# First stage of a two-layer decoder trunk: channel groups, another order of loads, and shift and scale columns ended on ScalarE

## The chip, the cores and the metric

One Trainium2 chip, one core. The time is the device time of one execution in microseconds (us); a profiled execution gives the trace. The kernel is Bass/Tile code in float32. A large product is made of three passes of a rounded type (fp32r): each operand is split into a high part and the remainder, and high x high, high x low and low x high are summed in PSUM. TensorE is PE in the profile, VectorE is DVE, ScalarE is ACT, GpSimd is POOL, and SyncE (SP), which issues nearly all DMAs, appears as SPq.

## The reference

What matters here is the head of layer 0. The conditioning vector c gives a shift and a scale for each of 1024 channels, x is modulated by them, and the result is projected:

```python
def ada_mod(c, w, b):
    m = (jax.nn.silu(c) @ w + b)[:, None, :]
    shift, scale, gate = jnp.split(m, 3, axis=-1)
    return shift, scale, 1.0 + gate
...
        shift, scale, gate = ada_mod(c, ada_w[layer, 0], ada_b[layer, 0])
        u = x * (1.0 + scale) + shift
...
            y = even_mixer(u, ev_w_in[e], ...)     # starts with proj = u @ w_in
```

x is 512 tokens x 1024 channels, the shift and scale columns of `ada_w` are 1024 x 2048 (8.4 MB), and the columns of `w_in` that the first stage multiplies are 640 of 2576, and 16 more. After it come the rest of the mixer, an MLP, an attention layer and another MLP, which the change does not touch.

## The kernel before, in words

`start` is the first stage. It goes through the 1024 channels in eight chunks of 128 (kc = 0 to 7). For a chunk, `load` issues on SyncE two DMAs of `ada_w` (tile `ast`, 512 KB each: z = 0 is the shift's columns, z = 1 the scale's, each with 128 columns for all 1024 rows), one of x (tile `x`, 256 KB) and, for every second chunk, one of `w_in` (tile `ws`, 640 KB for two chunks). `sums` makes silu(c) @ ada_w on VectorE: eight multiply-adds over the row blocks, alternating between two accumulators, and an addition (tile `mod`). `modulate` transposes x on TensorE (`pt`), sums the 128 partitions of `mod` by a product with ones (`pc`, a column of shift and one of scale), adds the bias on VectorE (`shift`, `scale`), and then on ScalarE makes u = x * scale + shift and its high part `uh`; GpSimd makes the low part `ul`. It ends with `split` of the next chunk's weights: `wh` on ScalarE, `wl` on GpSimd. `gemm(kc, 0)` is the five products of `wh` and `uh`, `gemm(kc, 1)` the twelve others, into five PSUM banks `pst` and one, `pz`.

The order of the work is written out by hand: `nc.order("tsvy")` chains the instructions of TensorE, ScalarE, VectorE and SyncE's DMAs in the order of the code, so that an instruction that waits holds up all behind it on its engine. GpSimd's order is the scheduler's. In the loop each step stands as: `load(kc + 3)`, three of the fifteen small parameter loads, `gemm(kc, 0)`, `modulate(kc + 1)`, `sums(kc + 2)`, `gemm(kc, 1)`. DMAs take eight completion semaphores in turn (named DMAHW0 to DMAHW7 in the rows of the order), so a DMA is issued only when the one eight places before it has landed. The tiles `ast` have four buffers to themselves, `ws` has two. After `start` the kernel takes weights of 1 MB each through the same two `ws` buffers (`w_dma`, `w_pre`).

Of the kernel before, what the change touches and what calls it, by code (L numbers as in the profile page):

```python
# [8 lines left out]
F32 = mybir.dt.float32  # L9
# [3 lines left out]
AF = mybir.ActivationFunctionType  # L13
# [60 lines left out]
class Trunk:  # L74
# [26 lines left out]
    def setup(self):  # L101
        nc, i, c = self.nc, self.i, self.const
        self.ident = c.tile([P, P], F32, name="ident")
        make_identity(self.tc.nc, self.ident)
        self.ones = c.tile([P, P], F32, name="ones")
        nc.vector.memset(self.ones, 1.0)
        self.ones_r = c.tile([P, P], F32R, name="ones_r")
        nc.vector.tensor_copy(self.ones_r, self.ones)
        self.eps = c.tile([P, 1], F32, name="eps")
        nc.gpsimd.memset(self.eps, LN_EPS)  # L110

        crow = c.tile([KC, P], F32, name="crow")
        nc.sync.dma_start(crow, i["c"].rearrange("o (k p) -> (o k) p", p=P))
        self.braw = self.s2("colB_raw")[:, :P]
        nc.scalar.dma_start(self.braw[:96], i["ada_b"].rearrange("l s (c p) -> (l s c) p", p=P))
        pc = self.ps()
        nc.tensor.transpose(pc[:, :KC], crow, self.ident[:KC, :KC])
        craw = c.tile([P, KC], F32, name="craw")
        nc.vector.tensor_copy(craw, pc[:, :KC])
        th = c.tile([P, KC], F32, name="cth")  # L120
        nc.scalar.activation(th, craw, AF.Tanh, scale=0.5)
        nc.vector.tensor_scalar(th, th, 0.5, 0.5, op0=ALU.mult, op1=ALU.add)
        self.cs = c.tile([P, KC], F32, name="cs")
        nc.vector.tensor_tensor(self.cs, th, craw, op=ALU.mult)

        self.shift, self.scale1 = {}, {}
        for n in range(4):
            self.shift[n] = c.tile([P, KC], F32, name=f"shift{n}")
            self.scale1[n] = c.tile([P, KC], F32, name=f"scale{n}")
        self.mod_d = {n: self.dram.tile([1, 2 * D], F32, name=f"modd{n}") for n in range(1, 4)}  # L130
        self.gate_d = {2: self.dram.tile([1, D], F32, name="gated2")}

    def ada_bias(self):
        nc, i, c = self.nc, self.i, self.const
        raw = self.braw
        pt = self.ps()
        nc.tensor.transpose(pt[:, :96], raw[:96], self.ident[:96, :96])
        self.colB = c.tile([P, 96], F32, name="colB")
        nc.vector.tensor_copy(self.colB, pt[:, :96])

    def param_loads(self):

# [437 lines left out]
    def start(self):  # L580
        nc, i = self.nc, self.i
        win = i["ev_w_in"][0]
        ada = i["ada_w"][0, 0]
        self.setup()
        self.new_u()
        acc_ps = [self.ps(f"pst{m}") for m in range(5)]
        pz = self.ps("pz")
        st, hl, mods = {}, {}, {}

        def load(kc):  # L590
            k0 = kc * P
            ast = self.u8(f"ast{kc}", F32, (2, KC, P))
            for z in range(2):
                nc.sync.dma_start(ast[:, z], ada[:, z * D + k0:z * D + k0 + P].rearrange("(r p) f -> p r f", p=P))
            xs = self.s2(f"x{kc}").rearrange("p (t f) -> p t f", t=NT)
            nc.sync.dma_start(xs, i["x"][0, :, k0:k0 + P].rearrange("(t p) f -> p t f", p=P))
            if kc % 2 == 0:
                wst = self.wp.tile([P, 2, 640], F32, tag="ws", bufs=WS_BUFS, name="ws")
                nc.sync.dma_start(wst, win[k0:k0 + 256, 0:640].rearrange("(k p) f -> p k f", p=P))
            else:  # L600
                wst = st[kc - 1][2]
            st[kc] = (ast, xs, wst)

        def sums(kc):

            ast = st[kc][0]
            mf = self.s2(f"mod{kc}")
            ma = mf.rearrange("p (a z f) -> p a z f", a=2, z=2)
            for z in (slice(0, 1), slice(1, 2)) if kc in (0, KC - 1) else (slice(0, 2),):
                for r in range(KC):  # L610
                    m, src, c = ma[:, r % 2, z], ast[:, z, r, :], self.cs[:, r:r + 1]
                    if r < 2:
                        nc.vector.tensor_scalar(m, src, c, None, op0=ALU.mult)
                    else:
                        nc.vector.scalar_tensor_tensor(m, src, c, m, op0=ALU.mult, op1=ALU.add)
            nc.vector.tensor_tensor(ma[:, 0], ma[:, 0], ma[:, 1], op=ALU.add)
            mods[kc] = ma

        def modulate(kc):
            xs = st[kc][1]  # L620
            pt = self.ps("pt")
            for t in range(NT):
                nc.tensor.transpose(pt[:, t * P:t * P + P], xs[:, t], self.ident)
            ma = mods.pop(kc)
            pc = self.ps("pc")
            for z in range(2):
                nc.tensor.matmul(pc[:, 2 * z:2 * z + 2], ma[:, 0, z], self.ones[:, 0:2], start=True, stop=True)
            nc.vector.tensor_tensor(self.shift[0][:, kc:kc + 1], pc[:, 0:1], self.colB[:, kc:kc + 1], op=ALU.add)
            nc.vector.tensor_scalar(self.scale1[0][:, kc:kc + 1], pc[:, 2:3], self.colB[:, 8 + kc:9 + kc], 1.0,
                                    op0=ALU.add, op1=ALU.add)  # L630
            u = self.s2("u32")
            sc, sh = self.scale1[0][:, kc:kc + 1], self.shift[0][:, kc:kc + 1]
            nc.scalar.activation(u, pt, AF.Identity, scale=sc, bias=sh)
            uh, ul = self.uk(kc)
            nc.scalar.copy(uh, u)
            nc.gpsimd.tensor_tensor(ul, u, uh.bitcast(F32), op=ALU.subtract)
            if kc + 1 < KC:
                split(kc + 1)

        def split(kc):  # L640
            wst = st[kc][2]
            hi = self.wp.tile([P, 640], F32R, tag="wh", name="wh")
            nc.scalar.copy(hi, wst[:, kc % 2])
            lo = self.wp.tile([P, 640], F32R, tag="wl", name="wl")
            nc.gpsimd.tensor_tensor(lo, wst[:, kc % 2], hi.bitcast(F32), op=ALU.subtract)
            hl[kc] = (hi, lo)

        def gemm(kc, part):
            hi, lo = hl.pop(kc) if part else hl[kc]
            uh, ul = self.uk(kc)  # L650
            a, z = kc == 0, kc == KC - 1
            ms = [slice(m * P, m * P + P) for m in range(5)]
            if part == 0:
# [10 lines left out]
        load(0)  # L664
        self.ada_bias()
        load(1)
        wz = self.const.tile([P, KC, 16], F32, name="wz")
        nc.sync.dma_start(wz, win[:, 2560:2576].rearrange("(k p) f -> p k f", p=P))
        load(2)
        nc.order("tsvy")  # L670
        split(0)
        sums(0)
        modulate(0)
        sums(1)
        wzs = self.const.tile([P, KC, 32], F32R, name="wzs")
        nc.vector.tensor_copy(wzs[:, :, 0:16], wz)
        nc.vector.tensor_tensor(wzs[:, :, 16:32], wz, wzs[:, :, 0:16].bitcast(F32), op=ALU.subtract)
        for kc in range(KC):
            if kc + 3 < KC:
                load(kc + 3)  # L680
            if kc == 0:
                loads = self.param_loads()
            for f in loads[3 * kc:3 * kc + 3]:
                f()
            if kc == KC - 2:
# [12 lines left out]
        return acc_ps, pz
# [843 lines left out]
```

## Time and profile before

| | us |
|---|---|
| median of 3 runs (1270.35 to 1271.96) | 1271.13 |
| the profiled execution, its own time | 1276.4 |
| its span | 1274.7 |
| TensorE busy in the span | 1226.4 |
| VectorE busy | 917.2 |
| ScalarE busy | 587.0 |
| GpSimd busy | 513.3 |

TensorE is busy 96% of the span; of the 48.3 us in which it isn't, some 20 lie in the first 70 us. The page's row of the granted clock and the windows below tell where TensorE ran at the lower of its two levels. A matmul's end is modelled, so where matmuls follow each other the start of one to the start of the next is the better measure.

### The profile page before, as it was taken

To read this page: it belongs to the slowest core of one execution; us is meant where nothing else is said; L and a number is where in the kernel's file an instruction comes from. 1 tells how busy PE (TensorE), PEld (TensorE's weight loads), DVE (VectorE), ACT (ScalarE), POOL (GpSimd) and SP (SyncE) were. 2 spreads that over 40 slices of the span, in tenths; PEclk is the share of its full clock that TensorE was granted. 3 is DMA by queue.
4 is the path that set the end of the run, shared out by engine and by line. 5 is a ranking of instruction groups with operands and counts; after the bars stand their busy time and mean duration, and the time that the engine had idled before them with its cause. 6 is when DMAs were issued, how large, how long until landed. Compare 5 with 4: busy or idle time off the path is not lost. (4 is left out here: it accounts for less than half of the span.)

```text
span 1274.7 us, 17852 instructions
## 1 busy us (share of the span) xinstructions
PE 1226.4 (96%) x6529; PEld 1044.1 (82%) x6529; DVE 917.2 (72%) x1470; ACT 587.0 (46%) x1028; POOL 513.3 (40%) x524
## 2 busy tenths in 40 slices
PE   5899899999999999999999999999899999999997
PEld 4687678888888888888999999887888788888886
DVE  7879887867878766879578878778767745543656
ACT  2376553453544443523666677752453332322321
POOL 3466421538312320376256557558438000000166
PEclk9899999999999999999999999999899999999999
DMA  9757414262775456524232232343261624232311
GB/s 282 213 198 262 169 63 157 96 225 74 248 255 195 162 198 231 178 87 118 83 101 84 67 93 67 109 165 100 83 232 67 214 66 132 71 114 81 133 33 66
DMA packets 131529, 177.51 MB, mean 139 GB/s; under 512 B 9270, under 2 KB 87764, under 8 KB 131442
## 3 DMA queue, kind: packets, MB, share of 16 engines
q1 hardware_dynamic: 131330, 176.33, 43.0%
q8 instruction: 51, 0.84, 0.3%
q14 instruction: 36, 0.29, 0.1%
q10 hardware_dynamic: 112, 0.05, 0.0%
HBM read 172.10 MB, written 4.26 MB: 138 GB/s over the span
## 5 line engine op out<-in xcount | busy, mean ns | idle before, releaser
L50 DVE TENSOR_TENSOR wl<-ws,wh 128x512 fp32r<-128x512 f32 (+1 forms) x255 | 269.8, 1083 | 69.4 <-ACT wh L50 64.7
L50 ACT CAST wh<-ws 128x1024 fp32r<-128x1024 f32 (+2 forms) x271 | 207.7, 808 | 202.1 <-PE p L50 81.4
L50 PE MATMUL p<-uh,wh 128*128 128x512 f32 (+1 forms) x576 | 206.2, 366 | 0.0
L50 PE MATMUL p<-uh,wl 128*128 128x512 f32 (+1 forms) x576 | 205.9, 365 | 0.0
L50 PE MATMUL p<-wh,hh 128*128 128x512 f32 (+1 forms) x516 | 201.0, 390 | 0.0
L50 PE MATMUL p<-wh,hl 128*128 128x512 f32 (+1 forms) x516 | 200.0, 388 | 0.0
L50 PE MATMUL p<-wl,hh 128*128 128x512 f32 (+1 forms) x516 | 199.9, 387 | 0.0
L50 PE MATMUL p<-ul,wh 128*128 128x512 f32 (+1 forms) x576 | 192.9, 366 | 0.0
L50 POOL TENSOR_TENSOR acc<-acc,ast 128x512 f32<-128x512 f32 x70 | 102.8, 1468 | 205.1 <-ACT ast L50 111.7
L50 DVE TENSOR_TENSOR h<-r 128x512 f32<-128x512 f32 x64 | 52.7, 826 | 125.9 <-ACT r L50 124.6
L50 PEld LDWEIGHTS p<-uh,wl 128*128 128x128 f32 x576 | 108.7, 189 | 17.6
L50 PEld LDWEIGHTS p<-uh,wh 128*128 128x128 f32 x576 | 108.6, 189 | 17.4
L50 PEld LDWEIGHTS p<-ul,wh 128*128 128x128 f32 x576 | 100.9, 189 | 17.3
L50 PEld LDWEIGHTS p<-wl,hh 128*128 128x128 f32 x516 | 96.9, 188 | 20.2 <-issue 0.5
L50 PEld LDWEIGHTS p<-wh,hh 128*128 128x128 f32 x516 | 96.9, 188 | 20.0 <-ACT hh L50 0.2
L50 PEld LDWEIGHTS p<-wh,hl 128*128 128x128 f32 x516 | 96.9, 188 | 19.9
L50 ACT ACTIVATE r<-p,colA 128x512 f32<-128x512 f32 x64 | 43.8, 685 | 148.4 <-PE p L50 148.1
L50 POOL TENSOR_TENSOR ws<-ws,gate 128x512 f32<-128x512 f32 x16 | 25.0, 1596 | 210.9 <-DMA ws<-in_mlp_w_dram 210.9
L50 DVE TENSOR_TENSOR Y<-Y,p 128x512 f32<-128x512 f32 x96 | 64.7, 680 | 41.0 <-PE p L50 40.3
L50 DVE SCALAR_TENSOR_TENSOR acc<-ast,cs,acc 128x512 f32<-128x512 f32 x70 | 83.8, 1198 | 14.2 <-DMA ast<-in_ada_w_dram 13.8
L50 ACT ACTIVATE ast<-ast,cs 128x512 f32<-128x512 f32 x70 | 49.8, 721 | 93.2 <-DMA ast<-in_ada_w_dram 91.1
L50 POOL TENSOR_TENSOR ul<-u,uh 128x512 fp32r<-128x512 f32 x32 | 44.5, 1403 | 82.8 <-ACT uh L50 70.0
(317 smaller groups left out, 2686.2 us busy)
## 6 DMA issues: line engine op xcount, KB each, us to landing
ws<-in_mlp_w_dram SPq DMA_DIRECT2D x64, 1024.0 KB
ast<-in_ada_w_dram SPq DMA_DIRECT2D x160, 256.0 KB
ws<-in_od_w_in_dram SPq DMA_DIRECT2D x16, 1024.0 KB
ast<-in_ada_w_dram SPq DMA_DIRECT2D x16, 512.0 KB
ws<-in_ev_w_in_dram SPq DMA_DIRECT2D x7, 1024.0 KB
ws<-in_ev_w_out_dram SPq DMA_DIRECT2D x4, 1024.0 KB
nf<-fd SPq DMA_DIRECT2D x16, 256.0 KB
ws<-in_od_w_out_dram SPq DMA_DIRECT2D x4, 1024.0 KB
```

What stands on the lines that cost most here:

```text
L50: x = f(*a, **k)
```

## The change

The eight chunks are loaded and summed in six groups: 0, 1, (2, 3), (4, 5), 6, 7. A group of two loads `ada_w` in rows of 256 columns instead of 128 (four DMAs of 512 KB into two tiles), x in rows of 256 channels, and sums with VectorE instructions of 512 elements a partition (shift and scale of two chunks) instead of 256. The shift of chunk 0 is not summed on VectorE: TensorE multiplies the eight row blocks as they were loaded with silu(c) (`cs2`). The bias additions leave VectorE: ScalarE makes each column of shift and scale from `pc` with the bias `colB` or `colB1` (bias plus one). Loads, sums, transposes, column sums and modulation become functions of their own, placed anew: the fifteen parameter loads stand together, behind group 3's loads and ahead of those of chunks 6 and 7.

```diff
+        self.cs2 = c.tile([P, KC, 2], F32, name="cs2")
+        for q in range(2):
+            nc.vector.tensor_tensor(self.cs2[:, :, q], th, craw, op=ALU.mult)
...
+        self.colB1 = c.tile([P, KC], F32, name="colB1")
+        nc.vector.tensor_scalar(self.colB1, self.colB[:, 8:16], 1.0, None, op0=ALU.add)
...
+        GROUPS = [(0,), (1,), (2, 3), (4, 5), (6,), (7,)]
...
+        def load(n):
+            g = GROUPS[n]
+            k0, w = g[0] * P, len(g) * P
+            nr = KC // len(g)
+            AST[n] = []
+            for r0 in range(0, KC, nr):
+                t = self.u8(f"ast{k0}_{r0}", F32, (2, nr, w))
+                for z in range(2):
+                    nc.sync.dma_start(t[:, z], ada[r0 * P:(r0 + nr) * P, z * D + k0:z * D + k0 + w]
+                                      .rearrange("(r p) f -> p r f", p=P))
+                AST[n] += [t[:, :, r] for r in range(nr)]
...
+        def sums(n):
+            w, zs = len(GROUPS[n]) * P, slice(0 if n else 1, 2)
+            ma = [self.s2(f"mod{n}")[:, 0:2 * w].rearrange("p (z f) -> p z f", z=2) for _ in range(2)]
+            for r in range(KC):
+                m, src, c = ma[r % 2][:, zs], AST[n][r][:, zs], self.cs[:, r:r + 1]
...
+        def columns(n):
+            pc, m = self.ps("pc"), mods.pop(n)
+            for q, kc in enumerate(GROUPS[n]):
+                for z in range(2):
+                    c0 = 4 * q + 2 * z
+                    if n or z:
+                        nc.tensor.matmul(pc[:, c0:c0 + 2], m[:, z, q * P:q * P + P], self.ones[:, 0:2],
+                                         start=True, stop=True)
                     else:
+                        for r in range(KC):
+                            nc.tensor.matmul(pc[:, c0:c0 + 2], AST[n][r][:, z], self.cs2[:, r],
+                                             start=(r == 0), stop=(r == KC - 1))
+                pcs[kc] = pc, 4 * q
...
         def modulate(kc):
-            nc.vector.tensor_tensor(self.shift[0][:, kc:kc + 1], pc[:, 0:1], self.colB[:, kc:kc + 1], op=ALU.add)
-            nc.vector.tensor_scalar(self.scale1[0][:, kc:kc + 1], pc[:, 2:3], self.colB[:, 8 + kc:9 + kc], 1.0,
-                                    op0=ALU.add, op1=ALU.add)
+            pc, c0 = pcs.pop(kc)
+            sc, sh = self.scale1[0][:, kc:kc + 1], self.shift[0][:, kc:kc + 1]
+            nc.scalar.activation(sh, pc[:, c0:c0 + 1], AF.Identity, bias=self.colB[:, kc:kc + 1])
+            nc.scalar.activation(sc, pc[:, c0 + 2:c0 + 3], AF.Identity, bias=self.colB1[:, kc:kc + 1])
...
+        sums(1)
+        load(3)
+        load_x(3)
+        load_w(4)
+        sums(2)
+        for f in self.param_loads():
+            f()
+        load(4)
+        load(5)
+        load_x(4)
+        load_x(5)
+        sums(3)
         for kc in range(KC):
+            n = of[min(kc + 1, KC - 1)]
+            new = kc + 1 < KC and GROUPS[n][0] == kc + 1
+            if kc == 2:
+                load_w(6)
+                sums(4)
+            if kc == 4:
+                sums(5)
                 self.w_dma()
             gemm(kc, 0)
             if kc + 1 < KC:
+                transposed(kc + 1)
+                if new:
+                    columns(n)
                 modulate(kc + 1)
-            if kc + 2 < KC:
-                sums(kc + 2)
             gemm(kc, 1)
```

On SyncE before, from the weights of chunks 6 and 7 to the last chunk's loads (`ast_419` and `x_422` are chunk 7's, `rawR` and `rawA` the parameter loads; the words in brackets are what a DMA waits for):

```order
L50 DMA ws<-in_ev_w_in_dram 128x2x640 [waits DMAHW4_49,Pool_49]
L50 DMA rawR<-in_od_q_norm_g_dram 1x64 [waits DMAHW5_49]
L50 DMA rawR<-in_od_k_norm_g_dram 1x64 [waits DMAHW6_49]
L50 DMA rawR<-in_od_b_f_dram 1x16 [waits DMAHW7_49]
L50 DMA ast_419<-in_ada_w_dram 128x8x128 [waits DMAHW0_49,DVE_49]
L50 DMA ast_419<-in_ada_w_dram 128x8x128 [waits DMAHW1_49]
L50 DMA x_422<-in_x_dram 128x4x128 [waits DMAHW2_49]
L50 DMA rawA<-in_ln_g_dram 32x128 [waits DMAHW3_49]
```

On SyncE now, from the end of group 3's loads (`x_219`, `ws`) to those of chunk 6 (`ast_0_252`) and chunk 7 (`ast_0_255`):

```order
L50 DMA x_219<-in_x_dram 128x2x256 [waits DMAHW6_49]
L50 DMA ws<-in_ev_w_in_dram 128x2x640 [waits DMAHW7_49,Pool_49]
L50 DMA rawR<-in_ev_conv_w_dram 16x128 [waits DMAHW0_49,Pool_49]
...
L50 DMA rawR<-in_od_q_norm_g_dram 1x64 [waits DMAHW7_49]
L50 DMA rawR<-in_od_k_norm_g_dram 1x64 [waits DMAHW0_49]
...
L50 DMA rawA<-in_ln_b_dram 32x128 [waits DMAHW5_49]
L50 DMA rawA<-in_mlp_b_dram 64x128 [waits DMAHW6_49]
L50 DMA ast_0_252<-in_ada_w_dram 128x8x128 [waits DMAHW7_49,DVE_49,PE_49]
L50 DMA ast_0_252<-in_ada_w_dram 128x8x128 [waits DMAHW0_49]
L50 DMA ast_0_255<-in_ada_w_dram 128x8x128 [waits DMAHW1_49,DVE_49]
```

All fifteen parameter loads stand between the weights of chunks 4 and 5 and chunk 6's `ast`; the eighth of them (`od_q_norm_g`) takes its semaphore behind those weights, and chunk 6's first `ast` takes it behind that small load.

On VectorE before, from the sums of chunk 2 (`mod_234`) to those of chunk 3:

```order
L50 SCALAR_TENSOR_TENSOR mod_234<-ast_140,cs,mod_234 128x256 x6
L50 TENSOR_TENSOR mod_234<-mod_234 128x256
L50 TENSOR_TENSOR shift_100<-pc,colB 128x1
L50 TENSOR_SCALAR scale_101<-pc,colB 128x1
L50 TENSOR_SCALAR mod_289<-ast_200,cs 128x256 x2
```

The same place now, from the end of chunk 1's sums (`mod_200`) through those of chunks 2 and 3 (`mod_223`):

```order
L50 TENSOR_TENSOR mod_200<-mod_200,mod_201 128x256
L50 TENSOR_SCALAR mod_223<-ast_0_145,cs 128x512
L50 TENSOR_SCALAR mod_224<-ast_0_145,cs 128x512
L50 SCALAR_TENSOR_TENSOR mod_223<-ast_0_145,cs,mod_223 128x512
...
L50 TENSOR_TENSOR mod_223<-mod_223,mod_224 128x512
L50 TENSOR_SCALAR mod_262<-ast_0_211,cs 128x512
```

Nothing that reads TensorE's `pc` stands between the sums any more; the sums of one group follow those of the group before.

## Rows read from the trace of the kernel before

**Rows 1.** Windows: stretch, length, PE, PEld, DVE, ACT, POOL busy, PEclk, DMA, GB/s.
```profile
2.50:46.00 43.50, 31.20 (x129) 23.54 (x130) 34.74 (x82) 11.84 (x18) 18.77 (x15) 0.92 1.16 304
52.50:57.00 4.50, 4.00 (x20) 2.91 (x18) 4.50 (x10) 1.97 (x3) 3.04 (x2) 1.00 0.00 0
60.43:63.84 3.41, 3.41 (x10) 2.37 (x9) 1.14 (x1) 3.16 (x4) 1.33 (x2) 0.50 0.47 156
70.00:1274.70 1204.70, 1176.11 (x6319) 1005.93 (x6317) 864.20 (x1348) 565.01 (x998) 480.11 (x486) 0.99 0.41 134
```
**Rows 2.** Timeline, TensorE's column sums and stage end: start, us, engine, instruction [idle before].
```profile
7.99 1.11 PE L50 MATMUL pt<-ident,x 128*128 128x128 f32 x4 [4.94 <-DMA x<-in_x_dram]
9.90 1.01 PE L50 MATMUL pc<-ones,mod 128*128 128x2 f32 x4 [0.81 <-DVE mod L50]
12.82 2.50 PE L50 MATMUL pst<-uh,wh 128*128 128x512 f32 x5 [1.90 <-ACT uh L50]
...
25.92 1.41 PE L50 MATMUL pst<-uh,wl 128*128 128x512 f32 x5
...
51.42 0.61 PE L50 MATMUL pc<-ones,mod 128*128 128x2 f32 x4 [2.22 <-DVE mod L50]
...
59.27 0.61 PE L50 MATMUL pc<-ones,mod 128*128 128x2 f32 x4 [2.77 <-DVE mod L50]
...
68.54 0.40 PE L50 MATMUL pz<-ul,wzs 128*32 128x512 f32 x1
```
**Rows 3.** Timeline, VectorE and GpSimd around the sums of chunks 1 and 2.
```profile
13.36 2.47 DVE L50 TENSOR_SCALAR mod<-ast,cs 128x256 f32<-128x256 f32 x2 [2.12 <-DMA ast<-in_ada_w_dram]
18.23 0.42 DVE L50 TENSOR_TENSOR mod<-mod 128x256 f32<-128x256 f32 x1
20.14 0.48 DVE L50 SCALAR_TENSOR_TENSOR mod<-ast,cs,mod 128x256 f32<-128x256 f32 x1
20.14 4.80 DVE L50 SCALAR_TENSOR_TENSOR mod<-ast,cs,mod 128x256 f32<-128x256 f32 x6
21.31 1.64 POOL L50 TENSOR_TENSOR ul<-u,uh 128x512 fp32r<-128x512 f32 x1 [5.34 <-ACT uh L50]
21.72 1.50 DVE L50 SCALAR_TENSOR_TENSOR mod<-ast,cs,mod 128x256 f32<-128x256 f32 x1
```
**Rows 4.** Timeline, the same kinds of instruction with nothing beside them.
```profile
10.47 1.53 POOL L50 TENSOR_TENSOR wl<-ws,wh 128x640 fp32r<-128x640 f32 x1 [9.00 <-ACT wh L50]
12.84 1.28 POOL L50 TENSOR_TENSOR ul<-u,uh 128x512 fp32r<-128x512 f32 x1 [0.84 <-ACT uh L50]
70.22 0.20 ACT L50 ACTIVATE lam<-lam 128x4 f32<-128x4 f32 x1
80.17 1.30 DVE L50 SCALAR_TENSOR_TENSOR y<-y,ay 128x512 f32<-128x512 f32 x2 [4.08 <-ACT ay L50]
```
**Rows 5.** Timeline, SyncE's issues, and the first use of what the first one loaded.
```profile
1.26 1.03 SPq L50 DMA_DIRECT2D ast<-in_ada_w_dram  x2
5.37 0.48 DVE L50 TENSOR_SCALAR mod<-ast,cs 128x128 f32<-128x128 f32 x2 [1.66 <-DMA ast<-in_ada_w_dram]
21.68 0.32 SPq L50 DMA_DIRECT2D rawR<-in_ev_conv_b_dram  x1
22.04 0.29 SPq L50 DMA_DIRECT2D rawR<-in_ev_rg_ba_dram  x1
22.37 1.26 SPq L50 DMA_DIRECT2D ast<-in_ada_w_dram  x2
43.16 0.81 SPq L50 DMA_DIRECT2D rawA<-in_ln_g_dram  x1
...
45.14 1.30 SPq L50 DMA_DIRECT2D EB<-in_ev_rg_wa_dram  x2
```
**Rows 6.** Windows with DMA rows of 512 bytes (first) and of 1 KB (second).
```profile
22.00:24.00 2.00, 2.00 (x8) 1.54 (x8) 2.00 (x2) 0.00 (x0) 2.00 (x2) 0.78 1.22 291
68.00:70.00 2.00, 2.00 (x11) 1.55 (x10) 0.28 (x2) 1.21 (x2) 2.00 (x6) 1.00 1.04 358
```

More of the change, by code (lines that the diff above doesn't have):

```diff
@@ L587, in start @@
         pz = self.ps("pz")
[L588 to L613, printed above, removed]
-                    else:
-                        nc.vector.scalar_tensor_tensor(m, src, c, m, op0=ALU.mult, op1=ALU.add)
-            nc.vector.tensor_tensor(ma[:, 0], ma[:, 0], ma[:, 1], op=ALU.add)
-            mods[kc] = ma
@@ L619, in modulate @@
-        def modulate(kc):
[L620 to L627, printed above, removed]
-            nc.vector.tensor_tensor(self.shift[0][:, kc:kc + 1], pc[:, 0:1], self.colB[:, kc:kc + 1], op=ALU.add)
-            nc.vector.tensor_scalar(self.scale1[0][:, kc:kc + 1], pc[:, 2:3], self.colB[:, 8 + kc:9 + kc], 1.0,
-                                    op0=ALU.add, op1=ALU.add)
+        AST, XS, WST, mods, hl, pts, pcs = {}, {}, {}, {}, {}, {}, {}
@@ new lines, in start @@
+        GROUPS = [(0,), (1,), (2, 3), (4, 5), (6,), (7,)]
+        of = {kc: n for n, g in enumerate(GROUPS) for kc in g}
+        def load(n):
[9 more added lines that the diff above has]
+                AST[n] += [t[:, :, r] for r in range(nr)]
@@ new lines, in load_x, with load_w @@
+        def load_x(n):
+            g = GROUPS[n]
+            k0, w = g[0] * P, len(g) * P
+            XS[n] = []
+            nt = NT // len(g)
+            for b in range(len(g)):
+                xs = self.s2(f"x{k0}").rearrange("p (t f) -> p t f", t=nt)
+                nc.sync.dma_start(xs, i["x"][0, b * nt * P:(b + 1) * nt * P, k0:k0 + w]
+                                  .rearrange("(t p) f -> p t f", p=P))
+                XS[n].append(xs)
+        def load_w(kc):
+            wst = self.wp.tile([P, 2, 640], F32, tag="ws", bufs=WS_BUFS, name="ws")
+            nc.sync.dma_start(wst, win[kc * P:kc * P + 256, 0:640].rearrange("(k p) f -> p k f", p=P))
+            WST[kc] = WST[kc + 1] = wst
@@ new lines, in sums @@
+        def sums(n):
[3 more added lines that the diff above has]
+                m, src, c = ma[r % 2][:, zs], AST[n][r][:, zs], self.cs[:, r:r + 1]
+                if r < 2:
+                    nc.vector.tensor_scalar(m, src, c, None, op0=ALU.mult)
+                else:
+                    nc.vector.scalar_tensor_tensor(m, src, c, m, op0=ALU.mult, op1=ALU.add)
+            nc.vector.tensor_tensor(ma[0][:, zs], ma[0][:, zs], ma[1][:, zs], op=ALU.add)
+            mods[n] = ma[0]
@@ new lines, in transposed @@
+        def transposed(kc):
+            n = of[kc]
+            nt, f = NT // len(GROUPS[n]), (kc - GROUPS[n][0]) * P
+            pts[kc] = self.ps("pt")
+            for t in range(NT):
+                nc.tensor.transpose(pts[kc][:, t * P:t * P + P], XS[n][t // nt][:, t % nt, f:f + P], self.ident)
+        def modulate(kc):
+            pc, c0 = pcs.pop(kc)
+            sc, sh = self.scale1[0][:, kc:kc + 1], self.shift[0][:, kc:kc + 1]
+            nc.scalar.activation(sh, pc[:, c0:c0 + 1], AF.Identity, bias=self.colB[:, kc:kc + 1])
+            nc.scalar.activation(sc, pc[:, c0 + 2:c0 + 3], AF.Identity, bias=self.colB1[:, kc:kc + 1])
@@ L631, in modulate @@
             u = self.s2("u32")
-            sc, sh = self.scale1[0][:, kc:kc + 1], self.shift[0][:, kc:kc + 1]
-            nc.scalar.activation(u, pt, AF.Identity, scale=sc, bias=sh)
+            nc.scalar.activation(u, pts.pop(kc), AF.Identity, scale=sc, bias=sh)
             uh, ul = self.uk(kc)
@@ L640, in split @@
         def split(kc):
-            wst = st[kc][2]
+            wst = WST[kc]
             hi = self.wp.tile([P, 640], F32R, tag="wh", name="wh")
@@ L664, in start @@
         load(0)
+        load_x(0)
+        load_w(0)
         self.ada_bias()
-        load(1)
         wz = self.const.tile([P, KC, 16], F32, name="wz")
         nc.sync.dma_start(wz, win[:, 2560:2576].rearrange("(k p) f -> p k f", p=P))
+        load(1)
+        load_x(1)
+        nc.order("tsvy")
         load(2)
-        nc.order("tsvy")
+        load_x(2)
+        load_w(2)
+        sums(0)
+        transposed(0)
+        columns(0)
         split(0)
-        sums(0)
         modulate(0)
-        sums(1)
         wzs = self.const.tile([P, KC, 32], F32R, name="wzs")
@@ L677, in start @@
         nc.vector.tensor_tensor(wzs[:, :, 16:32], wz, wzs[:, :, 0:16].bitcast(F32), op=ALU.subtract)
-        for kc in range(KC):
[L679 to L685, printed above, removed]
+        sums(1)
[10 more added lines that the diff above has]
+        sums(3)
+        for kc in range(KC):
+            n = of[min(kc + 1, KC - 1)]
[5 more added lines that the diff above has]
+                sums(5)
                 self.w_dma()
```

## The prediction

> **What bounds the kernel now.** I read the page first (TensorE busy 96%), then windows, to see where the other 4% lie, then the timeline of each engine over the first 70 us, and last SyncE's issues. From 70 us on TensorE is busy 1176.11 of 1204.70 us [rows 1]: there it sets the time, and what starts earlier ends earlier. In the first stage it works 31.20 of the 43.50 us from 2.5 to 46, while the DMAs run without a pause at 304 GB/s; but from 52.5 to 57 no DMA moves anything, VectorE is busy all the time, and the stage's last product starts only at 68.54 [rows 1, 2]. So the loads end well before the stage. What ends each wait of TensorE late in the stage is the sum of the next chunk on VectorE: it waits 2.22 us for `mod` before the column sums of chunk 6 (51.42) and 2.77 us before those of chunk 7 (59.27) [rows 2].
>
> Why VectorE is late the reader sees in chunk 2 [rows 3]. One multiply-add takes 0.48 us when alone; the one that starts at 21.72 beside GpSimd's `ul` (21.31, 1.64 us) takes 1.50. GpSimd's two instructions of a chunk take 1.28 and 1.53 us with nothing beside them [rows 4] and the first of them 1.64 here. The two engines take turns: VectorE loses nearly the time of GpSimd's instructions, 2.8 us a chunk. Six multiply-adds took 4.80 us for some 2.4 us of work. And the sums of chunk kc + 2 stand behind the bias additions of kc + 1, which wait for TensorE.
>
> **The change part by part.**
>
> Start. The tiny VectorE instructions for `cs2` and `colB1` fit in its 1.66 us of idleness before 5.37 [rows 5]: nothing. Chunk 0's shift on TensorE costs eight products in place of one. The trace shows two products of this kind as four records in 1.01 us at the lower clock level and in 0.61 us later [rows 2], so the eighteen records now cost 2.7 to 4.5 us. The nearest row is the first (same place, same level); as records overlap I take 3.8. They begin after the transposes (7.99 + 1.11, less overlap: 8.9) and end at 12.7, where the old ones ended at 10.9. The first product moves from 12.82 to some 14.7. Behind it wait chunk 0's `uh`, `ul` and GpSimd's split of chunk 1.
>
> Chunk 1. The 64 KB load `wz` now goes ahead of it: 0.2 to 0.5 us at 291 GB/s and below; I take 0.4, so its sums begin at 13.8 instead of 13.36. They ended at 18.65 (18.23 + 0.42) [rows 3]; as GpSimd's two instructions now fall wholly into them, up to 0.8 us more: 19.1 to 19.9, I take 19.6.
>
> Groups (2, 3) and (4, 5). Six multiply-adds of 512 elements at 0.65 us (two in 1.30 [rows 4]), two multiplications between 0.3 and 0.65, which I take at 0.45, and an addition of 0.65: 5.2 to 5.9, I take 5.5, for two chunks. With one chunk's GpSimd work within (2.8) each group takes 8.3 us. Their sums end at 27.9 and 36.2. Chunk 2 is later for it, but chunk 3 has no wait of its own and chunk 4 follows at 36.2.
>
> Loads. After chunk 1's `ada_w` (13.8) come x of chunk 1 (0.26 MB), then twice 2.62 MB of `ada_w` and x in rows of 1 KB and 0.66 MB of `ws`. Rows of 512 bytes move at 291 GB/s, rows of 1 KB at 358 [rows 6]: 0.9 + 2 x (7.3 + 1.8) = 19.1, so group 3's loads have landed at 33.0, ahead of their sums.
>
> The row of parameter loads is where I expect a new wait. A DMA is issued when the one eight places before has landed. The eighth small load stands behind the `ws` of chunk 4; only then can it and the seven after it go. Five cost 0.34 us each (21.68 to 22.04 to 22.37), the last three 1.98 together (43.16 to 45.14) [rows 5]: 3.6 us, during which nothing large is in flight. Then `ast` of chunk 6 is issued; the first `ast` of the kernel took 4.1 us from its issue to VectorE's first use (1.26 to 5.37 [rows 5]), the second half of it lands 512 KB later, 1.8 us. Chunk 6's sums can begin at 33.0 + 3.6 + 4.1 + 1.8 = 42.5, and VectorE, free at 36.2, waits 6 us for them. Chunk 7's loads follow at once, 46.1.
>
> Chunks 6 and 7. Two multiplications, six multiply-adds at 0.40 (4.80 less GpSimd's share is 2.4 for six) and an addition of 0.42 are 3.4 us, and two GpSimd instructions fall within: 42.5 + 3.4 + 2.8 = 48.7, against 51.42 before. Chunk 7: 3.4 and two or three GpSimd instructions (2.8 to 4.3), 54.9 to 56.4; I take 55.6, against 59.27: 3.7 us earlier.
>
> End. The two bias additions become two ScalarE instructions of 0.20 us [rows 4]; I cost the exchange at nothing (0.4 us either way), it is on the path once. After chunk 7's columns the work is the same as before, at the same lower clock level after TensorE's wait (0.50 from 60.43 to 63.84 [rows 1]), so the stage ends 3.7 us earlier, at 64.8. The next weights' first tile has long landed in the pause of rows 1, and the second is issued behind GpSimd's last split, which moves with the stage. Sum: -3.7 us. The profiled execution took 1276.4, 1.7 more than its span and 5.3 more than the median; 1276.4 - 3.7 = 1272.7, which is 1267.4 against the median of 1271.13.
>
> [...] The DMA rows show 291 GB/s for rows of 512 bytes and 358 for rows of 1 KB [rows 6]. [...]
>
> **The rivals.**
>
> The gap doesn't open (1264.0): SyncE gets through the small loads while group 3's data are still moving. For it: small DMAs have been issued 0.34 us apart beside running loads [rows 5]. Against it: the semaphore order given with the change. Then chunk 6's loads land by 36.7 and its sums end at 42.5, chunk 7's at 48.7, and TensorE itself becomes the bound. Its work for a chunk is 17 large products at 0.25 to 0.28 us (five in 1.41 [rows 2]), and transposes and columns of up to 1.2: 5 to 6 us. From chunk 4's columns at 36.3 there remain chunk 3's last twelve products (3.2) and four chunks: 59.5 to 63.5, I take 61.4, which is 7.1 us gained.
>
> The small loads are slow (1270.2): each takes the 0.8 us that the one at 43.16 took, eight of them 6.4 instead of 3.6. Chunk 6's loads land at 45.3, and 2.8 of the 3.7 us are gone. For it: SyncE's rows mix 0.3 and 0.8, and I can't see which is a wait.
>
> Wider rows bring nothing (1270.8): with 291 GB/s for the groups the loads land 2 x 2.62 x (3.44 - 2.79) = 3.4 us later, and 0.3 remains. Against it stands the row of 358.
>
> Slower (1275): SyncE comes to the small loads only when the queue is empty, so that all fifteen lie in the gap: at 0.8 us, 12 us instead of 3.6. It decides from the point where the gap is 3.7 us longer than my 3.6; fully there it costs 4.7 us on balance, 1275.8, and with a mixed pace about 1275. For it: `ws` of chunk 4 waits for GpSimd's split of chunk 1, which is late when chunk 0 is late, and all small loads stand behind it.
>
> **How the numbers follow.** Forecast (2.0 to 5.5 us gained) 0.54, no gap 0.16, slow small loads 0.13, no faster rows 0.05, slower 0.12. The forecast is 1267.4. Its own range is 1265.6 to 1269.1; with no gap at the lower end and the two cases of no change and the lighter part of the slower one at the upper, 1263.0 to 1273.0. A measurement of this kernel tells some 0.2%, 2.5 us, from no change. Faster by more: 0.50 of the forecast's 0.54 and 0.16, 0.66. Within: the other 0.04, 0.13 and 0.05, 0.22. Slower: 0.12.
>
> **What would show it.** In the profile after: sixteen records of column sums before chunk 0's ones, and the first product near 14.7 us; the sums of chunks 1 to 5 following each other on VectorE without a wait up to 36 us; an idle stretch of the DMAs between 33 and 38 us, with VectorE waiting for `ast` until 42; columns of chunk 6 near 48.7 and of chunk 7 near 55.7; the stage's last product near 64.8; and unchanged work after. It is wrong if the DMAs show no pause there, if chunk 6's columns come after 51, or if TensorE waits beyond 70 us where it did not before.

## The result, and the profile after

| | before | after |
|---|---|---|
| median of the runs, us | 1271.55 (6 runs, 1270.35 to 1275.05) | 1265.38 (6 runs, 1262.56 to 1268.15) |
| the profiled execution, us | 1276.4 | 1266.51 |
| its span | 1274.7 | 1264.8 |
| the stage's last product starts | 68.54 | 62.58 |

The ratio is 0.9949, 95% interval 0.993 to 0.9968: 6.2 us faster, where 3.7 were predicted. The sign and the place are as forecast, the size is not: 1265.38 lies just below the forecast's own range (1265.6 to 1269.1) and inside the whole one (1263.0 to 1273.0).

TensorE's timeline of the kernel after, over the first stage (start, us, engine, instruction, idle before it and what ended that), answers to [rows 2]:

```profile
7.42 1.11 PE L50 MATMUL pt<-ident,x 128*128 128x128 f32 x4 [4.35 <-DMA x<-in_x_dram]
8.33 3.41 PE L50 MATMUL pc<-cs,ast 128*128 128x2 f32 x16
11.60 0.57 PE L50 MATMUL pc<-ones,mod 128*128 128x2 f32 x2
14.13 2.50 PE L50 MATMUL pst<-uh,wh 128*128 128x512 f32 x5 [1.97 <-ACT uh L50]
...
46.43 0.58 PE L50 MATMUL pc<-ones,mod 128*128 128x2 f32 x4
...
53.33 0.61 PE L50 MATMUL pc<-ones,mod 128*128 128x2 f32 x4 [1.88 <-DVE mod L50]
...
62.58 0.40 PE L50 MATMUL pz<-ul,wzs 128*32 128x512 f32 x1
```

The eighteen column sums of chunk 0 stand at the front and the first product starts 1.31 us later than before. Chunk 6's columns no longer wait, chunk 7's still do. The last product comes 5.96 us earlier than in the profile before.

VectorE's timeline of the kernel after at the starts of chunk 1's sums, of group (2, 3)'s multiply-adds, and of chunks 6 and 7, answers to [rows 3]:

```profile
13.45 0.62 DVE L50 TENSOR_SCALAR mod<-ast,cs 128x256 f32<-128x256 f32 x2 [3.25 <-DMA ast<-in_ada_w_dram]
...
19.93 6.41 DVE L50 SCALAR_TENSOR_TENSOR mod<-ast,cs,mod 128x512 f32<-128x512 f32 x6
...
39.43 0.62 DVE L50 TENSOR_SCALAR mod<-ast,cs 128x256 f32<-128x256 f32 x2 [4.52 <-DMA ast<-in_ada_w_dram]
...
46.72 6.10 DVE L50 SCALAR_TENSOR_TENSOR mod<-ast,cs,mod 128x256 f32<-128x256 f32 x6
```

From chunk 1 to group (4, 5) VectorE has no wait, and then it stands still for 4.52 us until chunk 6's data land. Why shows in SyncE's issues of the kernel after, the first, the eighth and the last of the fifteen parameter loads that stand there and the load behind them (answers to [rows 5]), and in its windows (columns as in [rows 1]):

```profile
24.18 0.49 SPq L50 DMA_DIRECT2D rawR<-in_ev_conv_w_dram  x1
...
31.01 0.22 SPq L50 DMA_DIRECT2D rawR<-in_od_q_norm_g_dram  x1
...
33.28 0.56 SPq L50 DMA_DIRECT2D rawA<-in_mlp_b_dram  x1
33.95 3.89 SPq L50 DMA_DIRECT2D ast<-in_ada_w_dram  x4
```

```profile
2.50:46.00 43.50, 34.53 (x155) 27.87 (x156) 31.76 (x54) 14.84 (x32) 20.97 (x16) 1.00 0.95 311
...
30.00:32.00 2.00, 2.00 (x10) 1.54 (x9) 2.00 (x2) 1.02 (x4) 1.84 (x2) 1.00 0.06 20
32.00:34.00 2.00, 2.00 (x12) 1.61 (x11) 2.00 (x2) 1.23 (x2) 1.63 (x1) 1.00 0.06 15
...
54.20:57.60 3.40, 3.40 (x10) 2.47 (x9) 0.00 (x0) 3.33 (x6) 1.29 (x1) 0.50 0.96 327
70.00:1264.80 1194.80, 1167.93 (x6293) 999.00 (x6291) 859.89 (x1341) 561.41 (x992) 476.39 (x471) 0.99 0.41 134
```

The gap is there: the last of group 3's loads lands at 30.99, the eighth small load goes at 31.01, and the DMAs move 20 and 15 GB/s from 30 to 34 us while SyncE issues small loads one by one. TensorE works 34.53 us up to 46 instead of 31.20 [rows 1]. Behind chunk 7's wait it runs 3.4 us at a granted clock of 0.50, the lower of the two levels in the traces (0.50 and 1.00), as it did before (0.50 from 60.43 to 63.84 [rows 1]).

Why chunk 7's six multiply-adds take 6.10 us shows on ScalarE and GpSimd in that time:

```profile
46.80 0.73 ACT L50 CAST wh<-ws 128x640 fp32r<-128x640 f32 x1 [3.04 <-DMA ws<-in_ev_w_in_dram]
```

```profile
47.60 1.82 POOL L50 TENSOR_TENSOR wl<-ws,wh 128x640 fp32r<-128x640 f32 x1 [2.07 <-ACT wh L50]
49.38 1.48 POOL L50 TENSOR_TENSOR ul<-u,uh 128x512 fp32r<-128x512 f32 x1
50.83 1.71 POOL L50 TENSOR_TENSOR wl<-ws,wh 128x640 fp32r<-128x640 f32 x1
```

The weights `ws` of chunks 6 and 7 stand behind the small loads too. ScalarE waits 3.04 us for them, and so three GpSimd instructions fall beside chunk 7's sums. The gap thus reaches the stage's end by two ways: through the data of the sums, and through the time at which GpSimd works.

### The profile page after: what moved, and what is told of

It is laid out like the page before. It is cut to its first block, busy times and chain, and to the rows that moved or that the text cites. A ratio compares the mean times of both kernels' runs of the same rounds, so it can differ in the third digit from the quotient of the medians.

```text
span 1264.8 us, 17847 instructions
## 1 busy us (share of the span) xinstructions
PE 1224.6 (97%) x6543; PEld 1044.2 (83%) x6543; DVE 908.8 (72%) x1423; ACT 590.2 (47%) x1044; POOL 512.9 (41%) x524
```

## The experiments

Total times of such kernels scatter, so the stage's own end is the main measure: "last product" is the start of the stage's last TensorE product in the profile. It scatters as well, and most kernels have one profile: the kernel before has it at 68.54 and 67.66 in two profiles, and at 68.43 with 224 unused bytes a partition (before_pad224, below); late_params has 58.52 and 58.21. Differences below 0.9 us are not settled by it. The kernels ran on more than one chip, so medians are compared by their ratios.

| kernel | last product | median us | ratio to before, 95% |
|---|---|---|---|
| before_again | 67.66 | 1272.57 (1 run) | |
| before_pad | 67.28 | 1269.20 | 0.998, 0.9968 to 0.9992 |
| before_pad224 | 68.43 | 1272.04 (1 run) | |
| act_only | 62.51 | 1267.72 | 0.9964, 0.9951 to 0.9977 |
| act_only_pad | 61.66 | 1266.00 | 0.9949, 0.9933 to 0.9966 |
| vector_cols | 65.93 | 1265.63 | 0.9953, 0.9938 to 0.9968 |
| after | 62.58 | 1265.38 | 0.9949, 0.993 to 0.9968 |
| after_pad | 62.48 | 1265.14 | 0.9943, 0.9927 to 0.9959 |
| singles | 59.20 | 1264.27 | 0.9941, 0.9921 to 0.9961 |
| late_params | 58.52 | 1259.80 | 0.9908, 0.9892 to 0.9924 |
| late_params_again | 58.21 | 1260.19 | 0.9905, 0.9889 to 0.9922 |
| late_params_vshift0 | 58.13 | 1262.41 | 0.9925, 0.9905 to 0.9944 |
| no_wl | 58.17 | 1258.28 (1 run) | |

**The gap.** late_params moves one call in the kernel after:

```diff
-        for f in self.param_loads():
-            f()
         load(4)
...
                 load_w(6)
+                for f in self.param_loads():
+                    f()
```

> The kernel after, with the fifteen parameter loads moved from ahead of chunk 6's loads to behind the last w_in of the stage. Theory (the gap costs the rest of the gain): the loads of chunk 6 follow those of group (4, 5) at once and land near 34; the sums of chunk 6 run 35 to 42, of chunk 7 42 to 49; TensorE no longer waits 1.88 us ahead of chunk 7's columns, which come at 51.4, and it doesn't fall to the lower clock after them (about 1.7 us); the stage's last product starts at 59.0 to 60.7 in place of 62.58, and the time falls by 2 to 3.6 us to 1262-1263.5. Rival (TensorE's own work bounds the stage's end by now): chunk 7's columns at 51.4 and the stage's end no more than 1 us earlier, the time within 1 us of the changed kernel's. Second rival (the parameter loads are only pushed into the next wait): something behind the stage waits for EB or a parameter and the gain is lost there.

TensorE's timeline of late_params at chunk 7's columns and the last product, and its window over the former gap:

```profile
50.92 0.51 PE L50 MATMUL pc<-ones,mod 128*128 128x2 f32 x4
...
58.52 0.40 PE L50 MATMUL pz<-ul,wzs 128*32 128x512 f32 x1
```

```profile
30.00:32.00 2.00, 2.00 (x12) 1.54 (x11) 2.00 (x3) 0.74 (x3) 2.00 (x2) 1.00 1.15 347
...
54.00:58.00 4.00, 4.00 (x20) 3.18 (x19) 3.01 (x9) 2.20 (x3) 0.72 (x1) 1.00 0.67 229
```

The DMAs go on at 347 GB/s, chunk 7's columns wait for nothing, the granted clock stays at 1.00 through the stage's end (46 to 70 us). 4.06 us are gained: 1.88 of wait, 1.65 of lower clock (from chunk 7's columns to the last product it is 7.60 us here and 9.25 in the kernel after), and 0.5 in small steps ahead of them. The first theory holds; its 2 to 3.6 us were too few. The second rival costs 0.25 us at most: that is the first wait of TensorE behind the stage, at 64.17, for `at`, which GpSimd makes from such parameters.

**ScalarE's columns.** act_only is the kernel before with this alone; vector_cols is the kernel after with this alone undone (sums behind the modulation again):

```diff
-            nc.vector.tensor_tensor(self.shift[0][:, kc:kc + 1], pc[:, 0:1], self.colB[:, kc:kc + 1], op=ALU.add)
-            nc.vector.tensor_scalar(self.scale1[0][:, kc:kc + 1], pc[:, 2:3], self.colB[:, 8 + kc:9 + kc], 1.0,
-                                    op0=ALU.add, op1=ALU.add)
+            nc.scalar.activation(sh, pc[:, 0:1], AF.Identity, bias=self.colB[:, kc:kc + 1])
+            nc.scalar.activation(sc, pc[:, 2:3], AF.Identity, bias=self.colB1[:, kc:kc + 1])
```

> The kernel before, with one part of the change alone: ScalarE makes the columns of shift and scale from pc, so no VectorE instruction waits for TensorE any more. Theory (the gain is VectorE's freedom from TensorE): in the profile before, each of the five chunks 3 to 7 has some 0.95 us between the end of one sum and the start of the next on VectorE, in which it waits for pc; without it chunk 7's sums end near 54.5 in place of 59.2, and the stage's last product starts near 63.8 in place of 68.54: 4.7 us gained, nearly the whole gain of the change. Rival (the gain is the wider rows and VectorE's 512-element instructions): VectorE only waits elsewhere, for data, and the stage ends within 1.5 us of before.

TensorE's timeline of act_only at the columns of chunks 6 and 7 and at the last product:

```profile
49.47 0.61 PE L50 MATMUL pc<-ones,mod 128*128 128x2 f32 x4 [2.51 <-DVE mod L50]
...
54.84 0.61 PE L50 MATMUL pc<-ones,mod 128*128 128x2 f32 x4 [0.31 <-DVE mod L50]
...
62.51 0.40 PE L50 MATMUL pz<-ul,wzs 128*32 128x512 f32 x1
```

The theory holds: this part alone takes 5.15 us off the stage (67.66 to 62.51; 6.03 from the other profile of the kernel before), as much as the whole change (5.08 and 5.96). By the medians its ratio is 0.9964 and the whole change's 0.9949, with intervals that overlap. The rival falls.

> The kernel after, with the columns ended on VectorE again and the sums of a group behind the modulation of the chunk ahead of it, as before; groups, loads and chunk 0's shift stay. Reading the profile after: with pairs VectorE meets a column's wait only once a group, and chunk 6's sums wait for data until 39.4 anyway; only chunk 7's sums then start behind chunk 6's columns (46.43), near 47.3 in place of 46.2. Theory A (pairs and the data gap have taken most of what ScalarE's columns give): the stage's last product 1 to 1.5 us later than 62.58. Theory B (ScalarE's columns are the whole gain): the stage's last product at 66 to 68, as in the kernel before.

VectorE's timeline of vector_cols, the bias additions of group (2, 3) and of chunk 6, and TensorE's last product:

```profile
30.35 0.16 DVE L50 TENSOR_TENSOR shift<-pc,colB 128x1 f32<-128x1 f32 x1 [1.15 <-PE pc L50]
...
50.66 0.16 DVE L50 TENSOR_TENSOR shift<-pc,colB 128x1 f32<-128x1 f32 x1 [4.27 <-PE pc L50]
```

```profile
65.93 0.40 PE L50 MATMUL pz<-ul,wzs 128*32 128x512 f32 x1
```

3.35 us later than in the kernel after, 0.07 below the range of theory B and far above that of theory A. Theory A counted only chunk 7's wait; but VectorE waits at every group (1.03, 1.15, 1.77 and 4.27 us), TensorE's columns of chunks 4 and 5 come at 40.53 instead of 36.80, and from there TensorE's own work carries the delay on. The medians don't show the 3.35 us: the ratio is 0.9953 here and 0.9949 for the kernel after. The profiled execution was the slowest of this kernel's eight (1268.95).

**The start of the tiles.** The same first loads of `ada_w` ran faster in every changed kernel. before_again asks whether that was the execution:

> The kernel before once more, unchanged, beside the experiments on one chip. The open question is why the first 512-KB load of ada_w took 1.81 us in the profile before (5.27 to 7.08) and 1.50 us in the profile after (5.13 to 6.62), though it is the same load at the same place. If the two profiles only came from different executions or chips, this kernel shows about 1.50 us here (and with it loads that land earlier by up to a sixth, but a stage that ends where it did, 68.5, since VectorE and not the loads ended it). If the changed order of loads makes them faster, it shows 1.81 again.

It was 1.80 us there and in act_only too, on the chip that showed 1.50 in late_params: not the execution. One suspect in the diff is left: `cs2` and `colB1` add 96 bytes a partition ahead of every loaded tile. before_pad adds only such bytes to the kernel before, before_pad224 adds 224 and asks whether another multiple of 128 is as fast, after_pad adds 64 to the kernel after:

```diff
         self.setup()
+        self.const.tile([P, 24], F32, name="pad")
```

> The kernel before, with 96 unused bytes a partition among its constants. In the profiles of one chip the kernels before, before_again and act_only take 1.80 us from the landing of one 512-KB ada_w load to the next, and after, late_params and vector_cols take 1.50, for the same load into a tile of the same shape. The changed kernels have 96 bytes more of constants (cs2 64, colB1 32), so every later tile starts 96 bytes further on: ast of chunk 0 at byte 76,032 of a partition, a multiple of 128, in place of 75,936; in act_only it is 75,968, no multiple of 128 either. Theory (where a tile starts sets the rate of its loads): the second load of ada_w lands 1.50 us behind the first here too, chunk 1's two loads have landed near 12.0 in place of 13.2, and since VectorE's chain starts there and doesn't wait for data later, the stage's last product comes some 1.2 us earlier, 66.4 in place of 67.66. Rival (the order of the loads or the new tiles set the rate): 1.80 us as before, and nothing moves.

> The kernel before with 224 unused bytes a partition, so that ast starts at byte 76,160: a multiple of 128 but not of 256. The tiles that loaded at 345 GB/s in rows of 512 bytes start at 76,032, a multiple of both; those that loaded at 290 start at 75,936, 75,968 and 76,096, multiples of neither. [...]

> The kernel after, with 64 more unused bytes a partition among its constants, so that ast of chunk 0 starts at byte 76,096, no multiple of 128. Theory (where a tile starts sets the rate): 1.80 us from the first load's landing to the second's in place of 1.50, rows of 1 KB at 1.46 us or more for 512 KB in place of 1.36; group (4, 5)'s last load lands near 33 in place of 30.99, the sums of chunk 6 start near 41.4 in place of 39.4, and the stage's last product comes at 64 to 65 in place of 62.58: the prediction's 64.8. Rival: 1.50 us and 62.6.

Windows in which only rows of 512 bytes are loaded, of before_again (tiles from byte 75,936), before_pad (76,032) and before_pad224 (76,160); the last column is GB/s:

```profile
9.50:11.50 2.00, 1.01 (x4) 0.93 (x4) 0.56 (x3) 0.96 (x2) 1.10 (x1) 1.00 1.21 290
```

```profile
9.50:11.50 2.00, 1.02 (x4) 0.93 (x4) 0.38 (x3) 0.49 (x2) 1.54 (x1) 1.00 1.15 346
```

```profile
9.50:11.50 2.00, 1.01 (x4) 0.93 (x4) 0.63 (x3) 0.89 (x2) 1.04 (x1) 1.00 1.20 290
```

Windows with rows of 1 KB alone, of the kernel after (76,032) and of after_pad (76,096):

```profile
15.00:17.00 2.00, 2.00 (x7) 1.51 (x7) 2.00 (x2) 0.00 (x0) 2.00 (x2) 1.00 1.09 385
```

```profile
15.00:17.00 2.00, 2.00 (x6) 1.42 (x6) 2.00 (x2) 0.19 (x1) 2.00 (x2) 1.00 1.10 347
```

The start sets the rate: of the five starts only 76,032 was fast. 76,160 is a multiple of 128 as 76,032 is, and ran at 290 GB/s all the same. The traces show no addresses; the starting bytes are those of the built programs. By the shifts alone, tiles moved by 0, 32 and 224 bytes ran at 290 to 291 GB/s in rows of 512 bytes and by 96 at 346, and in rows of 1 KB tiles moved by 160 ran at 347 and by 96 at 385. Why 76,032 is the fast one, no run here shows. By these rates a row costs an estimated 4.5 ns more on its DMA engine if the tile starts elsewhere, for either of the two lengths: shared evenly, 512 KB are 64 rows of 512 bytes or 32 of 1 KB on each of the 16 DMA engines of the profile, (1.80 - 1.50) / 64 = 4.7 ns and (1.50 - 1.36) / 32 = 4.4.

What it gives in time is another matter. before_pad's chunk 1 starts at 11.97 instead of 13.28, but its last product comes only 0.38 us earlier than before_again's, not 1.2: chunk 2's columns come at 26.02 (25.76 in before_again), without a wait for `mod`, because TensorE is not there sooner, and chunk 3's sums stand behind them. By then nothing of the head start is left; later differences between such profiles (1.26 us to the first one of the kernel before) are not its doing. The granted clock is low at different places in them (0.50 from 60.43 to 63.84 us in the first profile of the kernel before; from 54.2 to 57.6 a mean of 0.65 in before_again and of 0.79 in before_pad); that this makes the differences is not shown. In after_pad everything up to chunk 6 is late as expected, and the stage's end is not. VectorE's timeline of after_pad at chunks 6 and 7, and TensorE's after it:

```profile
41.98 2.40 DVE L50 TENSOR_SCALAR mod<-ast,cs 128x256 f32<-128x256 f32 x2 [5.01 <-DMA ast<-in_ada_w_dram]
44.30 3.52 DVE L50 SCALAR_TENSOR_TENSOR mod<-ast,cs,mod 128x256 f32<-128x256 f32 x6
...
48.72 2.46 DVE L50 SCALAR_TENSOR_TENSOR mod<-ast,cs,mod 128x256 f32<-128x256 f32 x6
```

```profile
53.16 1.44 PE L50 MATMUL pst<-uh,wh 128*128 128x512 f32 x5 [1.28 <-ACT uh L50]
54.88 0.51 PE L50 MATMUL pc<-ones,mod 128*128 128x2 f32 x4
...
62.48 0.40 PE L50 MATMUL pz<-ul,wzs 128*32 128x512 f32 x1
```

Chunk 7's six multiply-adds take 2.46 us instead of 6.10, because GpSimd's work doesn't fall beside them (`ws` is issued later still, at 42.82 instead of 40.64, and GpSimd is busy for only 0.58 of the 2 us from 50 to 52); and TensorE's waits are 0.77, 0.47 and 1.28 us in three pieces, after which the granted clock stays at 1.00 (46 to 70 us).

> The kernel act_only (the kernel before, with ScalarE making the columns and nothing else of the change) with 64 unused bytes a partition, so that ast starts at byte 76,032, a multiple of 128. In act_only VectorE, free of TensorE, waits 6.9 us for ada_w in all, 3.3 of them in chunks 3, 4 and 6, and TensorE 2.51 us for chunk 6's sum. Theory (two lines do the work of the whole change: the columns on ScalarE and the start of the tiles): loads at 1.50 us for 512 KB, no wait of VectorE for data over 1 us after chunk 1's, and the stage's last product at 59.2 (singles, the same groups) to 60.5 in place of 62.51, which is earlier than the whole change has it (62.58). Rival (the three parameter loads a chunk and the four ast buffers hold the loads up, not their rate): VectorE still waits about 3 us, and the last product stays near 62.

TensorE's timeline of act_only_pad at chunk 6's columns and the last product:

```profile
47.60 0.61 PE L50 MATMUL pc<-ones,mod 128*128 128x2 f32 x4 [2.39 <-DVE mod L50]
...
61.66 0.40 PE L50 MATMUL pz<-ul,wzs 128*32 128x512 f32 x1
```

VectorE's waits for `ada_w` behind chunk 1's fall to 0.84 us, so the rate was the cause of those; but the last product gains 0.85 us, not the 2 to 3.3 expected. Chunk 6's sum is late for another reason: the sums of chunks 5 and 6 take 6.8 and 7.8 us, where chunk 7's without GpSimd's `wl` take 3.45 (45.37 to 48.82 in no_wl, below); turns with GpSimd fit that. Each side was half right.

**Groups, and chunk 0's shift.** singles sets `GROUPS = [(kc,) for kc in range(KC)]` in late_params, with the chunks loaded and summed in the same order:

> The kernel late_params with each chunk loaded and summed by itself (eight groups of one): rows of 512 bytes everywhere and VectorE instructions of 256 elements. What it keeps: ScalarE's columns, chunk 0's shift on TensorE, the parameter loads at the end, the start of the tiles. Theory (wide rows and wide instructions are worth nothing once VectorE is free of TensorE and tiles start where they do): loads at 340 GB/s, sums of a chunk some 3.5 + 2.8 us in turns with GpSimd, 6.3 each, chunk 7's at 13.5 + 7 x 6.3 = 57 at worst and about 51 where GpSimd's work is shared out as in act_only (38.5 to 54.8 for four chunks there); so the last product 58.5 to 61. Rival (the groups carry the gain: rows of 512 bytes are slower and VectorE's two multiplications and the addition cost once a chunk): loads at 291 GB/s, VectorE waiting for ast in most chunks as in act_only, the last product at 62 or later, the time 3 us or more above late_params.

TensorE's timeline of singles at chunk 6's columns and the last product:

```profile
46.71 0.61 PE L50 MATMUL pc<-ones,mod 128*128 128x2 f32 x4 [1.94 <-DVE mod L50]
...
59.20 0.40 PE L50 MATMUL pz<-ul,wzs 128*32 128x512 f32 x1
```

0.7 to 1.0 us of the stage, about as much as single profiles scatter: the groups are worth little once VectorE is free, which is the theory's side; the loads ran at 1.50 us for 512 KB and VectorE waited for none behind chunk 1's. The ratio, 0.9941 against 0.9908, is the rival's side and more than the stage explains; the two ran on different chips, and their intervals just overlap.

> The kernel late_params with chunk 0's shift summed on VectorE as before, no longer by TensorE. TensorE's sixteen products (3.41 us at 8.13) go, VectorE gets 2.1 us more ahead of chunk 1. Theory (that part of the change buys nothing): the stage's first product at 12.8 in place of 13.94, chunk 1's sums still start where its data land (13.2), the first later wait of TensorE for mod is longer by the same, and the last product stays at 58.5 within 0.4 us. Rival (it keeps VectorE free at the start): wzs comes later, chunk 1's columns 1 us or more later, and the last product with them.

The first product came at 12.72 and the last at 58.13, 0.1 to 0.4 us earlier than with TensorE's shift. That part of the change buys nothing that shows. The median is longer all the same, which is why late_params was run again:

> The kernel late_params once more, unchanged, beside act_only_pad: 1259.8 us was the median of four runs, and the same stage with one part undone (late_params_vshift0) took 1262.41 though its last product came 0.39 us earlier. If the medians of such kernels scatter by 2 to 3 us for reasons outside the stage, this run gives 1260 to 1263; if late_params really has 2.6 us on its neighbour, 1259.8 again. The stage's last product at 58.5 either way.

1260.19 us, last product at 58.21: late_params stays where it was. The 2.2 us between it and late_params_vshift0 don't come from the stage; as the two ran on different chips and their intervals overlap (0.9905 to 0.9944 against 0.9889 to 0.9922), it is not settled that they are real.

**Turns with GpSimd.** no_wl leaves GpSimd's `wl` out for chunks 1 to 7 (`lo = hi` in `split`).

> The kernel after, with GpSimd's low part of the weights (wl) left out for chunks 1 to 7; TensorE multiplies the high part in its place, so the low part of the weights is missing from the output. Theory (VectorE and GpSimd take turns): group (2, 3)'s six multiply-adds shrink from 6.41 us by about GpSimd's one instruction of 1.5 to 2.0, to 4.4-4.9, and again in group (4, 5); chunk 6's sums still start near 39 (the data gap), take some 5 us in place of 6.84, chunk 7's likewise, so the columns of chunk 7 come without a wait at or before 51.5 and the last product near 59 in place of 62.58 (1.88 us of wait and 1.65 of lower clock less). Rival (VectorE's multiply-adds are slowed by the DMAs writing, not by GpSimd): their durations and the stage's end stay.

VectorE's timeline of no_wl, chunks 6 and 7:

```profile
41.50 3.49 DVE L50 SCALAR_TENSOR_TENSOR mod<-ast,cs,mod 128x256 f32<-128x256 f32 x6
...
45.90 2.46 DVE L50 SCALAR_TENSOR_TENSOR mod<-ast,cs,mod 128x256 f32<-128x256 f32 x6
```

Chunk 7's six take 2.46 us instead of 6.10, group (4, 5)'s 1.41 + 3.17 instead of 6.41, and the last product comes at 58.17, without a wait at chunk 7's columns and at a granted clock of 1.00 (46 to 70 us), though chunk 6's data land as late as before (39.55). The theory holds, and its rival falls: the DMAs move 313 GB/s from 2.5 to 46 us, against 311 in the kernel after. The gap and GpSimd's turns each cost the kernel after some 4 us (4.06 and 4.41 at the last product): either one away, and chunk 7's sum is ready in time.

## Why the prediction was right, and where its size was off

The mechanism was right. VectorE's sums set the stage's end, they were held up by its waits for TensorE, the change frees them, and the row of small loads opens a gap that takes part of it back. Steps one by one, predicted and measured: first product 14.7, 14.13; chunk 1's sums 13.8 to 19.6, 13.45 to 19.2; groups' sums done at 27.9 and 36.2, 27.1 and 34.9 (7.85 us a group, not 8.3); group 3's loads landed 33.0, 30.99; chunk 6's sums from 42.5, 39.43; chunk 7's columns 55.7, 53.33; from there to the last product 9.1, 9.25.

The term that was mis-sized is the loads. "291 GB/s for rows of 512 bytes" [rows 6] was the rate of `ast` tiles that start at byte 75,936; the change starts them at 76,032, where rows of 512 bytes ran at 346 (before_pad) and rows of 1 KB at 385. The 358 GB/s taken for these was read from another tile (`ws`, behind the stage) and was no steady rate: that window opens as the load begins, and from 68.30 to 70 us it runs at 372. That 358 lies near the 347 of after_pad's `ast` is luck. after_pad, which undoes only this, has group 3's loads landed at 33.18 and chunk 6's sums from 41.98 to 48.27, against the predicted 33.0, 42.5 and 48.7. The gap itself was 8.4 us from the landing to chunk 6's sums, where 3.6 + 4.1 + 1.8 = 9.5 were counted. Together that makes chunk 6 start 3.1 us earlier than predicted; its sums took 0.6 longer, and 2.4 remained at chunk 7's columns. That is the sum for this run, but the loads alone don't decide the stage's end: after_pad has them as slow as predicted, and its last product comes at 62.48 all the same. There the term for chunk 7 was too large (3.4 us and two or three GpSimd instructions, 6.9 in all; 3.4 measured, 48.19 to 51.63), and the lower clock level behind chunk 7's columns ("the same lower clock level") didn't come: a granted clock of 1.00 (46 to 70 us) and 7.60 us to the last product, not 9.1.

Three points of the reasoning don't hold as they stand. A later landing was carried one for one to the stage's end; after_pad shows that it needn't be, since it also moves VectorE's sums against GpSimd's work. And the sum was made against one profile of the kernel before: its stage's end is 68.54 there and 67.66 in before_again, so the stage gave 5.1 to 6.0 of the 6.2 us. And the 1.01 us of the first column sums [rows 2] were put down to the lower clock level: the granted clock is 1.00 from 9.5 to 11.5 us in that trace, and why they take longer than the later 0.61 no run shows.

The rivals: no gap was put at 3.4 us better than the forecast; late_params shows 4.1 to 4.4 at the last product, and 5.2 to 5.6 by the ratios. TensorE as the next bound was right, but its work on a chunk is 4.8 us (46.12 to 50.92 in late_params), not 5 to 6. "Wider rows bring nothing" falls: 385 against 346. The slow small loads and the slower case fall: seven of the small loads were issued while group 3's data were still moving (24.18 to 29.41), and the others took 0.22 to 0.56 us each.

Part by part, by the last product: ScalarE's columns 5.2 to 6.0 us alone (3.35 if taken from the whole), the start of the tiles between -0.1 and 0.85 (1.26 if the first profile of the kernel before is taken), the groups 0.7 to 1.0, TensorE's shift nothing or a little less than nothing, and the place of the small loads minus 4.1 to 4.4. One part no run undoes alone: the kernel before sums chunk 7 in two halves, shift and scale, of 128 elements each, the changed ones in one go of 256. From the first multiplication to the addition that takes 4.05 us in act_only (49.34 to 53.39) and 3.01 in singles (46.58 to 49.59). The version that beats both kernels is late_params: 0.9908 (0.9892 to 0.9924) and again 0.9905 (0.9889 to 0.9922).

What stays open: the medians don't follow the stage to better than some 3 us. Beside the kernel before on the same chip vector_cols' median gains 6.8 us and before_pad's 2.8, where their stages gain 1.7 and 0.4 on before_again. So the 6.2 us of the whole change fit the 5.1 to 6.0 of its stage, but that they are the same is not shown. In single profiles the part behind the stage's last product took 1198.3 to 1206.2 us, and nothing in it was found that goes with one part of the change.

## What to carry to other kernels

An engine with its own queue of bulk work should not hold, in program order, a tiny instruction that waits for another engine: in act_only, moving two such instructions a chunk to ScalarE took as much off the stage as the whole change did. Before issuing a row of small loads, ask what is still in flight behind which they can hide; put them after the last large load that something waits for (late_params, 4.06 us at the last product). And a few bytes of new constants can shift every tile behind them (here 96 bytes, and 346 GB/s instead of 290): compare the rate of a load that the change does not touch before blaming or praising the new order.

## What the hardware showed that was not expected

Loads into `ast` tiles that start at byte 76,032 of the partition ran at 346 GB/s in rows of 512 bytes (before_pad) and at 385 in rows of 1 KB (the kernel after). Into tiles that start at 75,936, 75,968 and 76,160 rows of 512 bytes ran at 290 to 291 (before_again, act_only, before_pad224), into tiles that start at 76,096 rows of 1 KB at 347 (after_pad).

A wait of TensorE near 2 us late in the stage was followed by the lower clock level in some kernels and not in others. Behind the 1.88 us in the kernel after the granted clock is 0.50 from 54.2 on, and the stretch from chunk 7's columns to the last product takes 1.65 us longer (9.25 against 7.60). Behind the 1.60 us at chunk 6 in before_again it is 0.54, behind the 1.94 in singles and the 2.51 in act_only, also at chunk 6, it stays at 1.00 (windows in that order):

```profile
52.90:56.30 3.40, 3.40 (x10) 2.52 (x9) 3.40 (x12) 2.02 (x3) 1.65 (x2) 0.54 0.01 2
```

```profile
46.70:49.90 3.20, 3.19 (x16) 2.58 (x17) 3.17 (x9) 2.44 (x5) 0.59 (x1) 1.00 0.53 100
```

```profile
49.50:52.90 3.40, 3.40 (x17) 2.73 (x18) 3.40 (x15) 2.44 (x5) 0.82 (x1) 1.00 1.01 326
```

So the length of the wait alone doesn't decide; what does, no run here shows.
